# Windowed attention: the value products with a mixed base and stacked half-width corrections

## The chip, the cores and the metric

The kernel runs on one core of one Trainium2 chip. Its time is the device time of one execution in microseconds (us). The core has five engines with a queue of instructions each, worked off in order: PE (TensorE, matrix products; PEld is its weight load), DVE (VectorE), ACT (ScalarE), POOL (GpSimd) and SP (SyncE). In this kernel SP and POOL issue the transfers, which run on 16 DMA engines. The order of each queue is fixed when the program is built; semaphores hold an instruction back until what it reads is there and what it overwrites has been read.

## The reference

One inference step of a hybrid decoder layer for 1024 prompt tokens and 8 x 8 sample tokens with shared weights, all in float32. Cut to what matters here:

```
q, k, v, glu_a, glu_b, gate_a, gate_b = rmsnorm(x) @ w_in
A = attention(q, k, v) @ w_o_attn            # window 128, 16 heads of 64, 4 kv heads, sinks
B = swish(layernorm(conv31(glu_a * sigmoid(glu_b)))) @ w_pb
h = x + (sigmoid(gate_a) * A + sigmoid(gate_b) * B) @ w_out
y = h + ConvFFN(rmsnorm(h))                  # then a final rmsnorm

def swa_prompt(q, k, v, sinks):              # blocks of 128 queries
    # block n attends to the keys of block n-1 and of its own block n
    i, j = arange(128)[:, None], arange(256)[None, :]
    delta = i + 128 - j
    mask = (delta >= 0) & (delta < 128)      # exactly 128 keys for each query
    p = softmax(concat([where(mask, q k^T / 8, -inf), sink]))
    return p[..., :-1] @ v
```

Query i of a block sees the keys 0 to i of its own block and the keys i+1 to 127 of the block before. So each key position 0 to 127 is used exactly once, with one of the two blocks' key and value.

## The kernel before

A float32 product is made of three matmuls: weights and activations are split into a high and a low part (`split_ps`: a cast on ACT, a difference on DVE), and `mm3` (L208, L209, L210) adds high x high, high x low and low x high. The tokens (1024 + 64) stream through a weight in chunks of 384, 384 and 320 columns.

The program has phases. Phase x streams the weights of the input projection over the normed tokens: the convolution inputs (b, a), gates (g), then k, v and q, and between them runs the attention units. Eight units of the prompt (one for each block of 128 queries) and four of the samples are done for each pair p of key heads: p = 0 at about 205 to 366 us of the span, p = 1 at about 445 to 592 us. A unit has steps that hang on an agenda: `values` (the split of the values), and for each of two groups g of four heads `scores`, `turn` (transposes the probabilities p with four matmuls and splits them into `ph` and `pl`, 128 keys x 512 columns, that is 4 heads x 128 queries) and `mix` (the product with the values). `stream` calls `tick` ahead of each three matmuls, and a step is issued when its time on the agenda has come. So its matmuls stand between those of the stream. A scheduler of the framework then sets each engine's order by priorities and dependences.

The values of a block and of the one before meet in this way: `vt[:, 0]` holds the split values of the own block, `vt[:, 1]` the split difference v[blk-1] - v[blk]. `mix` multiplies p with the own values, and adds the product of the difference with that part of p whose key lies in the block before (key position j > i, a mask `below` on the transposed p). For block 0 there is no block before and no correction. With correction, two masked copies `pth0` and `ptl0` (L471, 128 x 512 each on DVE) and four matmuls of 512 columns (L482) are needed for each group, without it two. The corrected ones are 7 blocks x 2 groups x 2 pairs = 28 mixes. Sums of high and low part are taken later: the stationary operand `v` has the high values in one half of its columns and the low ones in the other, so the two halves of the output's partitions are added (L487 on ACT, L488 on DVE).

Beside this, the convolution module: `conv` runs 31 taps on DVE (L582 and others) for each of 8 channel tiles; its result goes to memory in the tile `d_c` by two transfers that POOL issues (L606 with 64 columns, L605 with 1024), and `ln_steps` (the LayerNorm of the branch) loads it back as `ct` (L634, SP), sums squares on DVE (L620) and takes the mean over channels with a matmul on PE (L628, `aux<-sm,mean`). The first such mean stands on PE near 629 us. The gates go out to `d_ga` and `d_gb` (POOL, L804) from `gt`, a copy of the PSUM bank on ACT (L240); they come back as `ga` (SP, L1064), and ACT takes their sigmoid (L1065). The finished attention of p = 0 lies in memory as `d_ah`, `d_al` and comes back as `ah`, `al` (SP, L1018 and L1019) into the space that the attention units leave.

A weight tile is loaded raw (`wraw`, SP, L157, two buffers) and split into `whi` and `wlo` (ACT L179 or L189, with L180 and an adding transfer of POOL, L181, or with DVE L190).

Of the kernel before, what the change touches and what calls it, by code (L numbers as in the profile page):

```python
# [129 lines left out]
class Build:  # L130
# [291 lines left out]
    def attn_unit(self, p, blk, st):  # L422
# [34 lines left out]
        def turn(g):  # L457
            pt = live[g]["pt"]
            ps = self.bank("aux")
            for h in range(4):  # L460
                nc.tensor.transpose(ps[:, h * P:(h + 1) * P], pt[:, h, 0:P], self.ident)  # L461
            ph = self.t(self.at, [P, 512], "pth", F32R)
            pl = self.t(self.at, [P, 512], "ptl", F32R)
            parts = [(0, ph), (0, pl)]
            with self.later(TURN_SOONER if self.now - self.gated <= 3 else 0):
                self.split_ps(ph, pl, ps)
                if blk:
                    below = self.masks[:, None, WIN:2 * WIN].to_broadcast([P, 4, WIN])
                    for x, tag in ((ph, "pth0"), (pl, "ptl0")):
                        x0 = self.t(self.at, [P, 512], tag, F32R)  # L470
                        nc.vector.tensor_tensor(x0.rearrange("p (a b) -> p a b", a=4),  # L471
                                                x.bitcast(F32).rearrange("p (a b) -> p a b", a=4), below, ALU.mult)
                        parts.append((1, x0))
            live[g]["parts"] = parts

        def mix(g):
            r, o = [slice(x * HD, (x + 1) * HD) for x in (g, 1 - g)]
            av = self.bank("aux")
            parts = live[g]["parts"]
            for n, (y, x) in enumerate(parts):  # L480
                v = vals["vt"][:, y, 2 * g:2 * g + 2, :].rearrange("p x d -> p (x d)")
                nc.tensor.matmul(av, v, x, start=n == 0, stop=n == len(parts) - 1)  # L482
            if g == 0:
                live[0]["t"] = self.t(self.at, [P, 4 * P], "av").rearrange("p (a b) -> p a b", a=4)
            t = live[0]["t"]
            av = av.rearrange("p (a b) -> p a b", a=4)
            nc.scalar.copy(t[r], av[o])  # L487
            nc.vector.tensor_tensor(t[r], av[r], t[r], ALU.add)  # L488
            if g == 1:
                self.split_ps(q[0][:, :, qs], q[1][:, :, qs], t)  # L490
# [239 lines left out]
    def phase_x(self):  # L730
# [129 lines left out]
        def do_v():  # L860
            ws = [self.weight(("v", 0)), self.weight(("v", 1))]
            for blk in range(9):
                c = min(blk // 3, 2)
                off = blk * P - CHUNKS[c][0] if blk < 8 else CHUNKS[2][1] - P
                ps = self.bank("mm")
                for k in range(KT):
                    wh, wl = ws[k // 4]
                    kk = slice((k % 4) * 256, (k % 4) * 256 + 256)
                    lh, ll = xh[c][:, k, off:off + P], xl[c][:, k, off:off + P]
                    self.mm3(ps[:, :256], lh, ll, wh[:, kk], wl[:, kk], k == 0, k == KT - 1)  # L870
                if blk < NBLK:
                    nc.scalar.copy(self.v[:, blk].rearrange("p x g d -> p (x g d)"), ps[:, :256])
# [127 lines left out]
        kv = pool(kv_es, "kv")  # L1000
        self.at = pool(kv_es, "at")
        self.v = self.t(kv, [P, NBLK, 2, 2, HD], "v")
        self.masks = self.t(kv, [P, MTOT], "masks")
        nc.sync.dma_start(self.masks, a["masks"])

# [1122 lines left out]
def pack_masks():  # L2128
# [10 lines left out]
    return np.concatenate([above, below, np.where(ok, 0.0, -1e30).astype(np.float32)], 1)  # L2139


def pack_consts(i):
# [81 lines left out]
```

## Time and profile before

| | |
|---|---|
| median of 3 runs | 1638.94 us (1638.71 to 1641.65) |
| profiled execution | 1639.45 us, span 1637.7 us, mean granted clock 0.998 |
| busy PE / DVE / ACT / POOL | 1621.8 / 1369.8 / 901.9 / 301.6 us |
| share of PE in the chain that ended last | 80% |
| idle PE, longest waits | 3.4 us at L628 (for DVE), 2.0 us at L209 (for a weight) |

The profile's times are microseconds from the start of the span. A row of the timeline has start, duration, engine, line, operation, out<-in, shape and number, and in square brackets how long the engine was idle before it and what released it. Matmuls overlap in the records, so their rate is read from the distance of their starts. "SPq" is SP's queue.

### The profile page before, as it was taken

The page shows a single profiled execution, that of the slowest core. Times are in us where ns is not written, and L with a number is a line of the kernel's source. Part 1 is how long each engine was busy: PE and PEld are TensorE (multiplying, and loading weights), DVE is VectorE, ACT ScalarE, POOL GpSimd, SP SyncE. Part 2 cuts the span into 40 slices and gives each one's busy share as a digit, 9 for nine tenths or more (in the row PEclk, how much of TensorE's full clock was granted, in tenths as well). Part 3 has the DMA queues.
Part 4 walks back from the last instruction along what each step waited for, and adds up shares of the span by engine and source line. Part 5 has one row for each costly group of instructions (what it writes and reads, how often), then busy time and mean ns, then how long its engine had stood idle before and what let it go on. Part 6 is the DMA issues. An engine that isn't in the chain of part 4 may idle for free.

```text
span 1637.7 us, 30023 instructions
## 1 busy us (share of the span) xinstructions
PE 1621.8 (99%) x11428; PEld 1602.6 (98%) x11428; DVE 1369.8 (84%) x2463; ACT 901.9 (55%) x1948; POOL 301.6 (18%) x587
## 2 busy tenths in 40 slices
PE   9999999999999999999999999999999999999998
PEld 9999999999999999999999999999999999999998
DVE  7889678999869996788755999988888877889767
ACT  6535387875588754576532465555555555524322
POOL 0210122333112221111102422322222111000000
PEclk9999999999999999999999999999999999999999
DMA  6343433545433366548763632344444334676423
GB/s 211 98 98 90 114 95 97 140 132 143 109 85 78 118 215 202 176 154 232 188 227 102 209 119 72 112 116 118 119 120 109 106 106 157 225 177 160 110 62 110
DMA packets 110329, 221.51 MB, mean 135 GB/s; under 512 B 26600, under 2 KB 57320, under 8 KB 110168
## 3 DMA queue, kind: packets, MB, share of 16 engines
q1 hardware_dynamic: 81528, 131.47, 26.0%
q0 software_dynamic: 28224, 87.71, 20.2%
q8 instruction: 90, 1.47, 0.4%
q14 instruction: 55, 0.45, 0.1%
q10 hardware_dynamic: 432, 0.40, 0.1%
HBM read 137.55 MB, written 64.03 MB: 123 GB/s over the span
## 4 chain that ended last, share of the span: by engine, by line
PE 80%; DVE 8%; DMA 4%; issue 4%; ACT 3%; POOL 0%; SPq 0%; POOLq 0%; DVEq 0%; ACTq 0%
PE mm L208 19%; PE mm L209 19%; PE mm L210 19%; PE aux L210 6%; PE aux L208 6%; PE aux L209 6%; DVE c L582 2%; PE aux L482 1%; DVE bt L582 1%; DVE q L824 1%; PE aux L461 1%; PE aux L449 1%; PE aux L450 1%; DMA ct<-d_c 1%; DMA wlo<-wraw 1%
## 5 line engine op out<-in xcount | busy, mean ns | idle before, releaser
L208 PE MATMUL mm<-xh,whi 128*128 128x384 f32 (+1 forms) x904 | 299.2, 331 | 0.2 <-ACT xh L297 0.2
L209 PE MATMUL mm<-xl,whi 128*128 128x384 f32 (+1 forms) x904 | 296.4, 328 | 0.4 <-DVE xl L298 0.4
L210 PE MATMUL mm<-xh,wlo 128*128 128x384 f32 (+1 forms) x904 | 296.3, 328 | 0.3 <-DMA wlo<-wraw 0.3
L209 PEld LDWEIGHTS mm<-xl,whi 128*128 128x128 f32 x904 | 170.5, 189 | 2.5 <-DVE xl L298 0.9
L208 PEld LDWEIGHTS mm<-xh,whi 128*128 128x128 f32 x904 | 170.5, 189 | 2.0 <-ACT xh L297 0.7
L210 PEld LDWEIGHTS mm<-xh,wlo 128*128 128x128 f32 x904 | 170.2, 188 | 1.1 <-DMA wlo<-wraw 0.7
L1470 DVE SCALAR_TENSOR_TENSOR acc<-st,fc,acc 128x1104 f32<-128x1104 f32 x88 | 119.8, 1364 | 12.2 <-issue 6.7
L582 DVE SCALAR_TENSOR_TENSOR bt<-u,consts,bt 128x513 f32<-128x513 f32 x120 | 89.6, 746 | 3.7 <-ACT bt L592 3.1
L210 PE MATMUL mm<-th,wlo 128*128 128x272 f32 x320 | 92.3, 289 | 0.0
L209 PE MATMUL mm<-tl,wlo 128*128 128x272 f32 x320 | 92.3, 288 | 0.0
L208 PE MATMUL mm<-th,wlo 128*128 128x272 f32 x320 | 92.2, 288 | 0.0
L582 DVE SCALAR_TENSOR_TENSOR c<-sm,hsum,c 128x512 f32<-128x512 f32 x120 | 89.3, 745 | 0.5
L210 PE MATMUL mm<-mh,wlo 128*128 128x272 f32 (+4 forms) x304 | 88.9, 292 | 0.0
L582 DVE SCALAR_TENSOR_TENSOR c<-u,consts,c 128x512 f32<-128x512 f32 x112 | 83.4, 744 | 0.4
L243 ACT CAST whi<-wraw 128x512 fp32r<-128x512 f32 x76 | 47.5, 625 | 62.7 <-PE aux L210 25.7
L1815 ACT COPY st<-mm 128x272 f32<-128x272 f32 (+2 forms) x132 | 43.5, 348 | 54.0 <-PE mm L210 53.8
L243 ACT CAST wlo<-wraw 128x512 fp32r<-128x512 f32 x76 | 47.3, 623 | 40.1 <-DVE wraw L1666 16.6
L1468 ACT ACTIVATE acc<-st,fc 128x1104 f32<-128x1104 f32 x44 | 57.6, 1315 | 14.9 <-DVE st L1771 11.8
L208 PE MATMUL aux<-mh,whi 128*128 128x272 f32 (+4 forms) x216 | 63.8, 295 | 0.0
L209 PE MATMUL aux<-ml,whi 128*128 128x272 f32 (+4 forms) x216 | 63.5, 294 | 0.0
L244 DVE TENSOR_TENSOR wlo<-wraw,wlo 128x512 fp32r<-128x512 f32 x76 | 52.7, 695 | 9.5 <-ACT wlo L243 9.3
L208 PEld LDWEIGHTS mm<-th,wlo 128*128 128x128 f32 x320 | 60.2, 188 | 0.0
(726 smaller groups left out, 5799.2 us busy)
## 6 DMA issues: line engine op xcount, KB each, us to landing
wraw<-wall SPq DMA_DIRECT2D x118, 512.0 KB, 3.8
wlo<-wraw POOLq DMA_DIRECT2D x37, 512.0 KB, 4.5
bw<-d_b SPq DMA_DIRECT2D x42, 272.0 KB, 3.9
d_b<-gd POOLq DMA_DIRECT2D x36, 272.0 KB, 6.1
d_b<-acc POOLq DMA_DIRECT2D x24, 272.0 KB, 4.7
ar<-wdn SPq DMA_DIRECT2D x32, 192.0 KB, 3.8
d_g<-acc POOLq DMA_DIRECT2D x10, 544.0 KB, 4.7
ga<-d_ga SPq DMA_DIRECT2D x8, 544.0 KB, 5.4
```

Source lines behind the costliest of these rows:

```text
L208: mm(ps, wh, xh, start=first, stop=False, skip_group_check=more)
L209: mm(ps, wh, xl, start=False, stop=False, skip_group_check=more)
L210: self.last_mm = mm(ps, wl, xh, start=False, stop=last, skip_group_check=more).ins
L243: self.cast = self.nc.scalar.copy(h, src).ins
L244: self.low = self.nc.vector.tensor_tensor(l, src, h.bitcast(F32), ALU.subtract).ins
L449: nc.tensor.matmul(ps[:, j, :], q[g][:, h, qs], kd[g][:, keys], start=True, stop=False)
L450: nc.tensor.matmul(ps[:, j, :], q[g][:, h, qs], kl[g][:, keys], start=False, stop=True)
L461: nc.tensor.transpose(ps[:, h * P:(h + 1) * P], pt[:, h, 0:P], self.ident)
L582: mac = lambda o, x, w: nc.vector.scalar_tensor_tensor(o, x, w, o, ALU.mult, ALU.add)
L1468: nc.scalar.activation(acc, st[:, 0:AW], AF.Identity, bias=fb(f), scale=fw(f, 0))
L1470: nc.vector.scalar_tensor_tensor(acc, st[:, k:k + AW], fw(f, k), acc, ALU.mult, ALU.add)
L1815: self.evicted = (add if second and n == 0 and j == 1 else op)(d, r(banks[bank, j]))
```

## The change

1. `do_v` makes a second copy of the values, `vw`: the keys 0 to 63 of a block from the own block and the keys 64 to 127 from the block before. For this each block's values are copied out of PSUM twice more, as 64 x 256 on ACT (14 more copies). The base `vt` of a corrected unit is the split of `vw[:, blk]`.
2. With that base, a query of the first half of a block (i < 64) is wrong only for keys j < 64 with j > i, and one of the second half only for keys j >= 64 with j <= i, there with the other sign. So each half of the queries needs a correction over 64 keys alone. The mask table holds this with signs.
3. The 64 rows that `ph` would leave empty take `pl`: `ptc` is the masked `ph` (one operation of 128 x 512), over whose unused half of the partitions the masked `pl` is written, for each query half from the other half of the partitions (two operations of 64 x 256). The queries are laid out half by half (x h q), and `mix` puts them back in order when it splits the result.
4. The difference is split into `vs`, and `two` holds each of its key halves in both halves of the partitions, brought there by four transfers from SBUF to SBUF per unit on SP (64 x 256 float32, 64 KB each; 56 in all).
5. `mix` now has two matmuls of 512 columns with the base (L487, L488) and two of 256 columns with `ptc` and `two` (L491), one for each half of the queries.
6. `do_a` asks for two weights ahead where the next weight is v.

```diff
 values():
-            vt = vals["vt"] = self.t(self.at, [P, 2, 4, HD], "vt", F32R, bufs=2)
-            self.split_ps(vt[:, 0, 0:4:3, :], vt[:, 0, 1:3, :], self.v[:, blk, p])
+            vt = vals["vt"] = self.t(self.at, [P, 4, HD], "vt", F32R, bufs=2)
+            self.split_ps(vt[:, 0:4:3, :], vt[:, 1:3, :], (self.vw if blk else self.v)[:, blk, p])
             if blk:
                 d = self.t(self.at, [P, 2, HD], "vd")
                 nc.vector.tensor_tensor(d, self.v[:, blk - 1, p], self.v[:, blk, p], ALU.subtract)
-                self.split_ps(vt[:, 1, 0:4:3, :], vt[:, 1, 1:3, :], d)
+                s = self.t(self.at, [P, 4, HD], "vs", F32R)
+                self.split_ps(s[:, 0:4:3, :], s[:, 1:3, :], d)
+                two = vals["two"] = self.t(self.at, [P, 2, 4, HD], "two", F32R, bufs=2)
+                for x in range(2):
+                    for y in range(2):
+                        nc.sync.dma_start(two[y * HD:y * HD + HD, x].bitcast(F32), s[x * HD:x * HD + HD].bitcast(F32))
 turn(g):
-                    below = self.masks[:, None, WIN:2 * WIN].to_broadcast([P, 4, WIN])
-                    for x, tag in ((ph, "pth0"), (pl, "ptl0")):
-                        x0 = self.t(self.at, [P, 512], tag, F32R)
-                        nc.vector.tensor_tensor(x0..., x..., below, ALU.mult)
-                        parts.append((1, x0))
+                    c = live[g]["c"] = self.t(self.at, [P, 2, 4, HD], "ptc", F32R)
+                    side = self.masks[:, WIN:2 * WIN].rearrange("p (x q) -> p x q", x=2)
+                    pick = lambda o, x, m: nc.vector.tensor_tensor(o, x.bitcast(F32), m, ALU.mult)
+                    pick(c, ph, side[:, :, None, :].to_broadcast([P, 2, 4, HD]))
+                    for x in range(2):
+                        r, o = [slice(y * HD, (y + 1) * HD) for y in (x, 1 - x)]
+                        pick(c[o, x], pl[r, x], side[r, x, None, :].to_broadcast([HD, 4, HD]))
 mix(g):
-            for n, (y, x) in enumerate(parts):
-                v = vals["vt"][:, y, 2 * g:2 * g + 2, :].rearrange("p x d -> p (x d)")
-                nc.tensor.matmul(av, v, x, start=n == 0, stop=n == len(parts) - 1)
+            nc.tensor.matmul(av, pair(vals["vt"]), flat(ph), start=True, stop=False)
+            nc.tensor.matmul(av, pair(vals["vt"]), flat(pl), start=False, stop=True)
+            if blk:
+                for x in range(2):
+                    nc.tensor.matmul(av[:, x * 256:x * 256 + 256], pair(vals["two"][:, x]),
+                                     live[g]["c"][:, x].rearrange("p h q -> p (h q)"), start=False, stop=True,
+                                     skip_group_check=True)
...
-            self.stream(("a", i), xs, a_evac(u))
+            self.stream(("a", i), xs, a_evac(u), ahead=1 + (self.order[self.w_used + 1][0] == "v"))
...
+                    for r in (slice(0, HD), slice(HD, P)):
+                        if 0 < blk + (r.start > 0) < NBLK:
+                            nc.scalar.copy(flat(self.vw, r), ps[r, :256])
...
-    above, below = [x.astype(np.float32) for x in (jj[:, :WIN] > ii, jj[:, :WIN] < ii)]
+    below = np.where(jj[:, :WIN] < HD, (jj[:, :WIN] < ii) & (ii < HD), -1.0 * ((jj[:, :WIN] >= ii) & (ii >= HD)))
```

The engines' orders are the same in both kernels up to the stream of the weight v. After it they move in these places; a row has the line, the operation, out<-in with the number of the tile, and the shape.

PE, one mix of the last block but one of p = 1 (`pth`, `ptl` are the split probabilities, `ptc` the stacked ones), before and after:

```order
L210 MATMUL mm_6370<-xh_23_107,wlo_754_6110 128x384
L482 MATMUL aux_6418<-pth_6347,vt_6306 128x512
L482 MATMUL aux_6418<-ptl_6348,vt_6306 128x512
L482 MATMUL aux_6418<-pth_797_6351,vt_6306 128x512
L482 MATMUL aux_6418<-ptl_798_6353,vt_6306 128x512
L208 MATMUL mm_6370<-xh_23_107,whi_753_6109 128x384
```

```order
L210 MATMUL mm_6463<-xh_23_107,wlo_756_6197 128x384
L487 MATMUL aux_6511<-pth_6440,vt_6393 128x512
L488 MATMUL aux_6511<-ptl_6441,vt_6393 128x512
L208 MATMUL mm_6463<-xh_23_107,whi_755_6196 128x384
L209 MATMUL mm_6463<-xl_24_108,whi_755_6196 128x384
L210 MATMUL mm_6463<-xh_23_107,wlo_756_6197 128x384
L208 MATMUL mm_6463<-xh_23_107,whi_755_6196 128x384
L209 MATMUL mm_6463<-xl_24_108,whi_755_6196 128x384
L491 MATMUL aux_6511<-ptc_6444,two_6401 128x256
L210 MATMUL mm_6463<-xh_23_107,wlo_756_6197 128x384
L491 MATMUL aux_6511<-ptc_6444,two_6401 128x256
```

The corrections have half the columns, and stand some rows later, between matmuls of the stream.

POOL, near the end of phase x, where the last tile of the convolution goes out (`d_c_59`) among the gates (`d_ga_60`), before and after:

```order
L181 DMA wlo_868_6794<-wraw_6684 128x1024
L804 DMA d_ga_60<-gt_6823 128x384
L606 DMA d_c_59<-u_5426 128x64
L605 DMA d_c_59<-u_5426 128x1024
L804 DMA d_ga_60<-gt_6851 128x384
L804 DMA d_ga_60<-gt_6879 128x320
```

```order
L181 DMA wlo_869_6893<-wraw_6783 128x1024
L815 DMA d_ga_60<-gt_6922 128x384
L815 DMA d_ga_60<-gt_6950 128x384
L617 DMA d_c_59<-u_5495 128x64
L616 DMA d_c_59<-u_5495 128x1024
L815 DMA d_ga_60<-gt_6978 128x320
```

The two transfers of the convolution now stand behind the second of the three gate pieces. On ACT the copy that this piece waits for (`gt_6851` before, `gt_6950` after) stands behind the two sigmoids of `ga` in both kernels.

PE, at the first mean of the LayerNorm (L628 before, L639 after), before and after:

```order
L208 MATMUL mm_6931<-xh_23_107,whi_867_6793 128x384
L209 MATMUL mm_6931<-xl_24_108,whi_867_6793 128x384
L210 MATMUL mm_6931<-xh_23_107,wlo_868_6794 128x384
L628 MATMUL aux_6960<-sm_6893,mean_79 128x272
L208 MATMUL mm_6959<-xh_25_109,whi_867_6793 128x320
L209 MATMUL mm_6959<-xl_26_110,whi_867_6793 128x320
```

```order
L208 MATMUL mm_7058<-xh_25_109,whi_868_6892 128x320
L209 MATMUL mm_7058<-xl_26_110,whi_868_6892 128x320
L210 MATMUL mm_7058<-xh_25_109,wlo_869_6893 128x320
L639 MATMUL aux_7059<-sm_6992,mean_79 128x272
L208 MATMUL mm_7058<-xh_25_109,whi_868_6892 128x320
```

The mean stood ahead of the first matmul of the chunk of 320 columns; now it stands behind fifteen of them. The second mean has moved back by thirteen rows, the third stands where it stood. On SP, one weight load that stood behind the loads of `ct` (L634 before, L645 after) now stands ahead of them, as well as the 56 transfers of `two`, which stand between the weight loads of the units.

More of the change, by code (lines that the diff above doesn't have):

```diff
@@ L489, in mix @@
             if g == 1:
-                self.split_ps(q[0][:, :, qs], q[1][:, :, qs], t)
+                order = lambda x: x[:, :, qs].rearrange("p h (x q) -> p x h q", x=2)
+                self.split_ps(order(q[0]), order(q[1]), t.rearrange("p (x h q) -> p x h q", x=2, h=4))
             if p == 0 and g == 1 and blk in (3, 7):
@@ L1002, in phase_x @@
         self.v = self.t(kv, [P, NBLK, 2, 2, HD], "v")
+        self.vw = self.t(kv, [P, NBLK, 2, 2, HD], "vw")
         self.masks = self.t(kv, [P, MTOT], "masks")
@@ L2132, in pack_masks @@
     ii, jj = r[:, None], np.arange(2 * WIN)[None]
-    above, below = [x.astype(np.float32) for x in (jj[:, :WIN] > ii, jj[:, :WIN] < ii)]
+    above = (jj[:, :WIN] > ii).astype(np.float32)
+    below = np.where(jj[:, :WIN] < HD, (jj[:, :WIN] < ii) & (ii < HD), -1.0 * ((jj[:, :WIN] >= ii) & (ii >= HD)))
     b, t = r // HD, r % NT
@@ L2138, in pack_masks @@
     ok = np.concatenate([past] + new, 1)
-    return np.concatenate([above, below, np.where(ok, 0.0, -1e30).astype(np.float32)], 1)
+    return np.concatenate([above, below.astype(np.float32), np.where(ok, 0.0, -1e30).astype(np.float32)], 1)
 def pack_consts(i):
```

19 lines of the change are left out of this document (9 added, 10 removed).

## The prediction

> **What bounds the kernel.** I read the page's first part, then its chain by engine, then the waits of PE.
>
> ```profile
> span 1637.7 us, 30023 instructions
> PE 1621.8 (99%) x11428; PEld 1602.6 (98%) x11428; DVE 1369.8 (84%) x2463; ACT 901.9 (55%) x1948; POOL 301.6 (18%) x587
> PE 80%; DVE 8%; DMA 4%; issue 4%; ACT 3%; POOL 0%; SPq 0%; POOLq 0%; DVEq 0%; ACTq 0%
> PE aux L628 <- DVE sm L620: 4.7, 2, 3.4
> PE mm L209 <- DMA wlo<-wraw: 2.0, 1, 2.0
> ```
>
> PE is busy for 99% and carries 80% of the chain, so columns taken from PE count, unless PE waits for the same event afterwards. Its two longest waits are one for a weight (2.0 us) and one of 3.4 us at the first LayerNorm mean (L628), after all attention. All that PE saves in the attention units meets that second wait, so the question is whether its event comes earlier too.
>
> **PE's saving.** The price of a matmul is the distance of starts, here of 512 columns (three distances in the four rows from 566.99 to 567.66) and of 256 columns (five distances from 565.64 to 566.23).
>
> ```profile
> 565.64 0.28 PE L450 MATMUL aux<-kl,q 128*128 128x256 f32 x1
> 566.23 0.28 PE L449 MATMUL aux<-kd,q 128*128 128x256 f32 x1
> ...
> 566.99 0.39 PE L482 MATMUL aux<-pth,vt 128*128 128x512 f32 x1
> 567.66 0.47 PE L482 MATMUL aux<-ptl,vt 128*128 128x512 f32 x1
> ```
>
> 0.67 / 3 = 0.223 us for 512 columns and 0.59 / 5 = 0.118 us for 256. A corrected mix saves 2 x (0.223 - 0.118) = 0.21 us, 28 of them 5.9 us, half in each pair's units. The issue of the four matmuls stays. [...]
>
> **What DVE gets.** Before, a corrected group has two masks of 128 x 512 (L471); after, one of 128 x 512 and two of 64 x 256. The nearest row for a half-wide operation is the select of 128 x 256 (L454, two of them from 567.50 to 568.16).
>
> ```profile
> 566.29 0.68 DVE L471 TENSOR_TENSOR pth<-pth,masks 128x512 fp32r<-128x512 f32 x1
> 566.89 0.68 DVE L471 TENSOR_TENSOR ptl<-ptl,masks 128x512 fp32r<-128x512 f32 x1
> 567.50 0.77 DVE L454 COPY_PREDICATED p<-masks,aux 128x256 f32<-128x256 uint32 x2
> 568.16 0.68 DVE L244 TENSOR_TENSOR ptl<-aux,pth 128x512 fp32r<-128x512 f32 x1
> ...
> 472.00:613.60 141.60, 141.26 (x886) 136.32 (x885) 138.22 (x267) 104.47 (x288) 30.43 (x55) 1.00 0.46 131
> ```
>
> A mask costs 0.60 us, two halves 2 x 0.33 = 0.66. That is +0.06 us a mix, +0.8 us in the second pair's 14 mixes; between nothing and 2 x 0.60 for two halves lie -0.6 and +0.6 us a mix, and I keep +0.06, the nearest shape. It matters because of the last row (third busy time: DVE): from 472 to 613.6 us DVE works 138.2 of 141.6 us, and by overlapping records even less is free. So in the second pair PE may run ahead of DVE by 2.95 us only as far as its products then don't wait. In the rows above the last mask ends near 567.5 and its product starts at 567.66, 0.2 us later. After the change the corrections stand five and more rows of 0.17 us behind, which gives about 0.9 us. I take for PE's lead at the end of the attention, 592 us, the value of 5 us: 2.95 of the first pair, which DVE's backlog follows, and two thirds of the second. The ends are 3 and 5.9 us.
>
> ACT's 14 copies of 64 x 256 in the stream of v cost at most one such copy each, 0.38 us, and the row before them shows 2.48 us idle. The split of the difference is only renamed. The 56 transfers of 64 KB come to 3.6 MB.
>
> ```profile
> 197.61 0.38 ACT L872 COPY v<-mm 128x256 f32<-128x256 f32 x1 [2.48 <-PE mm L210]
> wraw<-wall SPq DMA_DIRECT2D x118, 512.0 KB, 3.8
> SPq L1018 <- PE aux L542: 5.1, 1, 5.1
> 595.00:620.00 25.00, 24.67 (x150) 24.34 (x149) 18.62 (x30) 6.71 (x9) 5.34 (x9) 1.00 1.04 350
> ```
>
> That is the volume of seven weight loads among 118, spread over 250 us; I cost them at nothing, with a transfer's 3.8 us for each unit hidden by the whole unit between `values` and `mix`. Should SP hold them behind a weight load that waits for its buffer, that cover is gone (a rival below). `ahead` of two at v moves no row, so it costs nothing; PE's 2.0 us wait for a weight stays.
>
> **What the first LayerNorm mean hangs on.** The chain of waits runs from the convolution's last write to the mean.
>
> ```profile
> 613.92 6.43 DMA d_c<-u
> 620.37 0.37 SPq L634
> 620.79 6.46 DMA ct<-d_c
> 627.37 0.74 DVE u L620
> 629.05 1.24 PE aux L628 x2
> ```
>
> Before, the write starts when DVE ends (613.6) and takes 6.43 us, in a stretch in which the DMA engines are full (the row from 595 to 620: share 1.04, 350 GB/s). That burst is `ah`, `al` and `ga`, and it begins when PE's last sample product lets go of the space (the wait of SP for `aux` L542). After the change, POOL has the write behind the second piece of the gate.
>
> ```profile
> 620.07 1.11 ACT L1065 ACTIVATE ga<-ga 128x1088 f32<-128x1088 f32 x1 [1.23 <-DMA ga<-d_ga]
> 621.09 0.46 ACT L240 COPY gt<-mm 128x384 f32<-128x384 f32 x1
> 621.84 0.54 POOL L804 DMA_DIRECT2D d_ga<-gt  x1 [7.38 <-ACT gt L240]
> 613.92 0.54 POOL L605 DMA_DIRECT2D d_c<-u  x1 [1.26 <-DVE u L603]
> 622.52 1.23 DVE L190 TENSOR_TENSOR wlo<-wraw,whi 128x1024 fp32r<-128x1024 f32 x1 [8.90 <-ACT whi L189]
> d_c<-u POOLq DMA_DIRECT2D x8, 512.0 KB, 2.9
> ```
>
> That piece went out at 621.84, since its copy on ACT waits out both sigmoids, and these the loads of `ga`. So the write is now released by the gate's load, not by DVE. The burst of loads starts 5 us earlier with PE, so the second piece goes out at 616.8, and after it and the small write (0.55 us each) the big write starts at 617.9: 4.0 us later than before. But by then the burst is over. The write takes between 2.9 us (the median of eight) and 6.43; I take 3.5, nearer the median, because one or two weight loads still run. It lands at 621.4 instead of 620.35. On SP a weight load that waits for DVE's L190 now stands ahead of `ct`; it was free at 623.75, 1.9 us after the second piece went out, so by the same shift at 618.7, before the write lands, and costs nothing unless the write is quick. The mean's operand is ready at 629.05 + 1.05 = 630.1.
>
> PE gets there earlier, but now with fifteen matmuls of 320 columns ahead.
>
> ```profile
> 625.35 0.34 PE L210 MATMUL mm<-xh,wlo 128*128 128x384 f32 x1
> 629.05 1.24 PE L628 MATMUL aux<-sm,mean 128*128 128x272 f32 x2 [3.36 <-DVE sm L620]
> 630.36 0.47 PE L209 MATMUL mm<-xl,whi 128*128 128x320 f32 x1
> 630.62 0.47 PE L210 MATMUL mm<-xh,wlo 128*128 128x320 f32 x1
> ...
> 633.07 0.31 PE L209 MATMUL mm<-xl,whi 128*128 128x320 f32 x1
> 633.80 0.31 PE L208 MATMUL mm<-xh,whi 128*128 128x320 f32 x1
> 692.90 0.72 PE L628 MATMUL aux<-sm,mean 128*128 128x272 f32 x2 [1.37 <-DVE sm L620]
> 647.11 1.05 ACT L189 CAST whi<-wraw 128x1024 fp32r<-128x1024 f32 x1 [5.49 <-PE mm L209]
> ```
>
> From 633.07 to 633.80 five distances give 0.146 us each, fifteen rows 2.2 us. PE would come to the mean at 625.7 - 5 + 2.2 = 622.9 and wait 7.2 us instead of 3.4. The sum at this place: the mean 1.05 us later, 2.2 us of work already done, net **1.15 us earlier**. The slow stretch stays: after 3.36 us without work two matmuls stand 0.26 us apart (630.36, 630.62), and from 633.07 on at the latest 0.146; I take the stretch as equally long after the longer wait. [...] The later means follow: the row at 647.11 shows the LayerNorm's ACT work behind a cast that waits for PE, so the chain takes PE's time there; the wait at 692.90 (1.37 us) moves with it.
>
> The sum: 1639.45 - 1.15 = 1638.3 for an execution like the profiled one. The profile lies 0.5 us over the median of 1638.94, so against it **1637.8 us**.
>
> **Rivals.** 0.2% is 3.3 us, about what a measurement of this kernel can tell from no change.
> (B) The saving arrives whole. The DMA queue drains faster than I assume, or the write needs no more than its 2.9 us, and the mean is no later than before by PE's own lead: 1638.94 - 5.9 = 1633.0, with a share of it up to 1635.6. For it speaks that `ga` was late only through the burst; against it that the write has to stand behind the gate, whose time is bounded by PE's lead, and that with the longest lead it lands at 619.9, 0.5 us earlier than now, for 0.5 + 2.2 = 2.7 us in all, 1636.2.
> (C) Slower through the gate: lead only 3 us, the second piece at 618.8, the big write at 619.9 with 6.43 us. It lands at 626.4, 6 us late, less 2.2: 3.8 us slower, 1642.7. It decides from a landing 5.5 us later than 620.35 (3.3 slower). For it: the order on POOL; against it: the burst is then over.
> (D) Slower through `two`: the corrections wait for a transfer or for DVE. The stall must exceed 0.21 us in a mix to lose the gain, and 1.15 + 3.3 = 4.5 us over 14 units, 0.3 us each, would make it slower beyond the noise: 1642.2 and more. PE shows no wait at its mixes before, but DVE has 0.2 us to spare at some.
> (E) The half matmul is no cheaper than two thirds of the full one (0.15 us): saving 28 x 2 x 0.07 = 4 us, PE's lead 3.4; the gate then holds the mean as in my sum with 1.6 us more, 1639.4, no change.
>
> **Chances.** My forecast 0.53, (B) 0.20, (C) 0.09, (D) 0.09, (E) 0.09. All of (B) but a tenth is faster by over 3.3 us and a few of my own case, together 0.23; (C) and (D) count half or more as slower, 0.13; the rest, 0.64, is the same. The range from 1633.6 to 1642.2 leaves out the lower half of (B) and the upper ends of (C) and (D). My own case alone spans 1636.2 (above) to 1640.7 (a write of 6.43 us with the lead of 5: 4.0 late, less 2.2).
>
> **What would show it.** Right: L491 at 0.118 us a row; no waits of PE in 205 to 592 us; the first mean with a wait for DVE of 5 to 9 us, released by the write of `d_c` that POOL issues right behind `d_ga`, at 617 to 619 us; later means within 1 to 2 us of before. Wrong: that mean's wait no longer than before (B), PE waiting at L491 for `two` or `ptc` (D), or the write of `d_c` landing after 625 us (C).

## The result and the profile after

The change made the kernel slower: 1649.93 us (median of 4 runs, 1647.94 to 1651.76) against 1638.83 for the kernel before (4 runs now), a ratio of 1.0064 with a 95% interval of 1.0050 to 1.0078. The forecast was 1637.8. Lines of the changed kernel's page, and below the break the longest waits of its PE:

```profile
span 1648.6 us, 30225 instructions
PE 1623.6 (98%) x11428; PEld 1600.2 (97%) x11428; DVE 1378.0 (84%) x2491; ACT 912.3 (55%) x1965; POOL 305.6 (19%) x587
PE 71%; DVE 13%; DMA 5%; issue 5%; ACT 5%; SPq 1%; POOL 1%; DVEq 0%; POOLq 0%; ACTq 0%
...
PE aux L550 <- ACT av L545: 5.3, 1, 5.3
PE aux L639 <- DVE sm L631: 5.2, 3, 3.7
PE aux L466 <- ACT p L420: 2.6, 1, 2.6
PE aux L488 <- DVE ptl L244: 1.7, 2, 1.4
```

The span grew by 10.9 us. DVE's busy time grew by 8.2 us, PE's share of the chain fell from 80 to 71%, and three waits of PE inside the attention units are new: 5.3 us for ACT's `av`, 2.6 us for the first softmax of the second pair, 1.7 us for `ptl`. The old wait at the LayerNorm mean is still there. So the time was lost where the forecast had PE running ahead: the same matmul of the stream (L208) that started at 592.43 us before now starts at 603.95.

**The halves on DVE.** Timeline of DVE in the changed kernel, then the group of all halves from 205 to 600 us:

```profile
477.94 0.68 DVE L475 TENSOR_TENSOR ptc<-pth,masks 128x512 fp32r<-128x512 f32 x1
478.54 0.28 DVE L399 CUSTOM_DVE_ANT_0 sp<-aux,masks,nm 128x64 f32<-128x64 f32 x1
478.86 0.87 DVE L475 TENSOR_TENSOR ptc<-ptl,masks 64x256 fp32r<-64x256 f32 x2
479.76 0.43 DVE L785 TENSOR_TENSOR u<-mm,u 128x256 f32<-128x256 f32 x1
...
L475 DVE TENSOR_TENSOR ptc<-ptl,masks 64x256 fp32r<-64x256 f32 x56 | 23.5, 420 | 1.7
```

The two halves take 479.76 - 478.86 = 0.90 us, 0.45 each, where the forecast had 0.33. The whole mask that they replace took 0.60. That is 0.30 us for each of 28 mixes, 8.4 us. Besides, the first half starts 0.04 us after the operation before it has ended (478.54 + 0.28 = 478.82), where the whole mask let its successor start 0.08 us before its own end (478.54 against 478.62). Over all 28 pairs this is another 0.11 us each, as picks_not_crossed shows below, so 0.41 us a mix or 11.5 us in all. DVE's busy time, which doesn't count the short pauses between the halves, grew by 8.2 us.

**The transfers of the difference.** ACT in the changed kernel, then PE, then SP's issue of the four transfers, then the wait of ACT summed from 195 to 600 us, and the window after (its last but two number is the granted clock):

```profile
485.53 0.62 ACT L243 CAST q<-av 128x512 fp32r<-128x512 f32 x1
492.48 0.30 ACT L243 CAST vs<-vd 128x128 fp32r<-128x128 f32 x1 [6.32 <-DMA two<-vs]
492.68 0.37 ACT L545 COPY av<-aux 128x256 f32<-128x256 f32 x1
...
493.10 0.80 PE L550 MATMUL aux<-av,vs 128*128 128x128 f32 x2 [5.26 <-ACT av L545]
...
483.40 4.37 SPq L443 DMA_DIRECT2D two<-vs  x4
...
ACT vs L243 <- DMA two<-vs: 15.0, 4, 6.3
...
493.00:500.00 7.00, 6.90 (x38) 6.90 (x39) 5.92 (x13) 5.09 (x20) 1.28 (x2) 0.76 0.18 67
```

The scheduler let `values` run units ahead, as far as buffers allow: the cast at 492.48 belongs to the unit two ahead of the next mix. The cast of `vs` (one buffer) waits until the transfers have read the last `vs`; these could not start before 483.40, when PE had done the last correction that still read the buffer of `two` to be written. Then they took 6.3 to 7.8 us from issue to landing, against a median of 2.4 us for all 56, in a stretch in which the DMA engines were 91 to 97% busy (483 to 489 us) and the adding transfer of a weight, 512 KB, had been issued at 482.08. Behind the cast in ACT's queue stands the copy `av` of a sample unit, and PE waits for that one. After 5.26 us of waiting PE's clock was 0.76 over the next 7 us, another 0.24 x 7 = 1.7 us: it was 0.50 from 493.5 to 496 us and 1.00 from 496.5 to 500. In the kernel before, after the 3.36 us of waiting at the mean, it was 0.50 from 630 to 632 and 1.00 from 633 to 636.

### The profile page after: what moved, and what is told of

Read it like the earlier page. It is cut to its first block, busy times and chain, and to the rows that moved or that the text cites. A ratio compares the mean times of both kernels' runs of the same rounds, so it can differ in the third digit from the quotient of the medians.

```text
span 1648.6 us, 30225 instructions
## 1 busy us (share of the span) xinstructions
PE 1623.6 (98%) x11428; PEld 1600.2 (97%) x11428; DVE 1378.0 (84%) x2491; ACT 912.3 (55%) x1965; POOL 305.6 (19%) x587
## 4 chain that ended last, share of the span: by engine, by line
PE 71%; DVE 13%; DMA 5%; issue 5%; ACT 5%; SPq 1%; POOL 1%; DVEq 0%; POOLq 0%; ACTq 0%
PE mm L208 16%; PE mm L209 16%; PE mm L210 16%; PE aux L210 6%; PE aux L208 6%; PE aux L209 6%; DVE c L593 4%; DVE bt L593 2%; DVE q L835 1%; DMA two<-vs 1%; DMA ct<-d_c 1%; DMA wraw<-wall 1%; ACT ct L673 1%; PE aux L454 1%; ACT p L416 1%
## 5 line engine op out<-in xcount | busy, mean ns | idle before, releaser
L208 PE MATMUL mm<-xh,whi 128*128 128x384 f32 (+1 forms) x904 | 299.1, 331 | 0.0
L208 PEld LDWEIGHTS mm<-xh,whi 128*128 128x128 f32 x904 | 170.7, 189 | 0.7 <-ACT xh L297 0.2
L208 PE MATMUL mm<-th,wlo 128*128 128x272 f32 x320 | 92.2, 288 | 0.0
L208 PE MATMUL aux<-mh,whi 128*128 128x272 f32 (+4 forms) x216 | 63.8, 295 | 0.0
L208 PEld LDWEIGHTS mm<-th,wlo 128*128 128x128 f32 x320 | 60.2, 188 | 0.0
```

Source lines behind the costliest of these rows:

```text
L208: mm(ps, wh, xh, start=first, stop=False, skip_group_check=more)
```

## The experiments

All ratios are to runs of the kernel before on the same chip.

| run | median us | ratio to before (95%) |
|---|---|---|
| pe_alone | 1636.34 | 0.9986 (0.9978 to 0.9995) |
| dve_alone | 1645.90 | 1.0049 (1.0037 to 1.0061) |
| vs_two_buffers | 1650.54 | 1.0068 (1.0053 to 1.0082) |
| four_half_picks | 1654.69 | 1.0100 (1.0086 to 1.0113) |
| two_three_buffers | 1649.52 | 1.0065 (1.0051 to 1.0078) |
| picks_on_pool | 1670.05 | 1.0194 (1.0176 to 1.0211) |
| picks_not_crossed | 1643.29 (one run) | |
| no_transfers | 1643.32 | 1.0027 (1.0018 to 1.0036) |
| held_back | 1647.32 | 1.0062 (1.0049 to 1.0074) |
| full_mask | 1653.73 | 1.0095 (1.0081 to 1.0108) |
| held_and_full | 1641.38 | 1.0022 (1.0013 to 1.0031) |
| moved_by_transfer | 1652.32 | 1.0087 (1.0073 to 1.0100) |
| no_transfers_full_mask | 1635.51 | 0.9980 (0.9971 to 0.9988) |
| held_one_less | 1642.56 | 1.0027 (1.0018 to 1.0036) |
| moved_by_act | 1650.44 | 1.0079 (1.0066 to 1.0091) |
| stacked_by_act | 1645.35 | 1.0049 (1.0035 to 1.0063) |

**pe_alone: only the matmuls.**

```diff
-                nc.tensor.matmul(av, v, x, start=n == 0, stop=n == len(parts) - 1)
+                w = slice(0, 256 if y else 512)
+                nc.tensor.matmul(av[:, w], v, x[:, w], start=n == 0, stop=n > 0, skip_group_check=y > 0)
```

> The kernel before, but each correction matmul covers only the left 256 of its 512 columns (this leaves out the correction of two of the four heads); DVE, ACT, POOL and SP have the same work as before. Theory A (PE's saving is real, the changed kernel lost it elsewhere): 56 matmuls cheaper by 0.10 us save up to 5.9 us on PE, of which the first LayerNorm mean may take back half: 1633 to 1636.5. Rival B (a matmul of 256 columns beside matmuls of 384 costs 0.18 us, as some rows of the changed kernel suggest): 2.5 us at most, 1636.5 to 1638. Rival C (PE's saving is worth nothing because DVE sets the end of the attention): 1638.5 to 1639.5.

Measured: 0.14% faster, 2.3 us of 1638.94, at the edge between theory A's range and rival B's. The price decides for A. A correction in this run, between matmuls of the stream, when its mask is long done:

```profile
563.69 0.34 PE L210 MATMUL mm<-xh,wlo 128*128 128x384 f32 x1
563.87 0.28 PE L483 MATMUL aux<-pth,vt 128*128 128x256 f32 x1
563.98 0.34 PE L208 MATMUL mm<-xh,whi 128*128 128x384 f32 x1
```

It costs 0.11 us, and the median of all 56 (from a correction's start to the start of the next matmul) is 0.118 us, the price forecast. So 256 columns are half the price. The matmul that started at 592.43 us before starts 4.6 us earlier here, near the forecast's lead of 5. POOL and PE at the LayerNorm's mean in the same run:

```profile
616.16 0.54 POOL L805 DMA_DIRECT2D d_ga<-gt  x1 [9.66 <-ACT gt L240]
617.23 0.54 POOL L606 DMA_DIRECT2D d_c<-u  x1
...
629.57 1.25 PE L629 MATMUL aux<-sm,mean 128*128 128x272 f32 x2 [6.22 <-DVE sm L621]
```

Here too the write of `d_c` stands right behind the second gate piece, at 617.23, and PE waits 6.22 us for the mean. This is the forecast's middle part as it was worked out (617.9 and 7.2 us): PE comes earlier, and the mean takes half or more of it back. The order changed here without the change's other parts, by the matmuls alone.

**dve_alone: only more work on DVE.**

```diff
                         parts.append((1, x0))
+                    more = self.t(self.at, [P, 256], "more")
+                    nc.vector.tensor_tensor(more, pl[:, 0:256].bitcast(F32), ph[:, 0:256].bitcast(F32), ALU.mult)
```

> The kernel before, with one more operation of 128 x 256 on DVE behind each pair of masks, written to a tile that nobody reads: 28 x 0.33 = 9.2 us of DVE, about the 8.2 us by which DVE's busy time grew in the changed kernel, and nothing else of the change. Theory A (DVE is the second bound, its work delays the convolutions and with them the second pair's first softmax and the first LayerNorm mean): 1642 to 1648. Rival (DVE had the room, the loss is all in the transfers of the difference): 1638 to 1640.

Measured: 0.49% slower, 7.0 us between the medians, of 9.2 us of added work. Theory A. The way it takes is seen at the end of the sixth convolution, which DVE must finish before the second pair's first softmax. First that row before; then in the changed kernel, with PE's wait for the softmax; then in dve_alone, with PE's waits at the LayerNorm means:

```profile
441.05 0.68 DVE L603 TENSOR_TENSOR u<-c 128x512 f32<-128x512 f32 x1
```

```profile
449.40 0.68 DVE L614 TENSOR_TENSOR u<-c 128x512 f32<-128x512 f32 x1
...
456.33 1.21 PE L466 MATMUL aux<-consts,p 128*128 128x128 f32 x4 [2.64 <-ACT p L420]
```

```profile
449.11 0.69 DVE L605 TENSOR_TENSOR u<-c 128x512 f32<-128x512 f32 x1
...
PE aux L630 <- DVE sm L622: 8.5, 4, 4.8
```

DVE is 8 us late there in both; PE itself is late by 1.5 us there in the changed kernel and by 2.5 in dve_alone, of which 2.0 came with a wait for a weight at 180.81 us, before any unit. The softmax behind it is late, and PE waits for the turn, 2.64 us in the changed kernel and 1.4 in dve_alone; at the LayerNorm means dve_alone waits 8.5 us instead of 4.7.

**vs_two_buffers and two_three_buffers: more buffers.** `vs` gets `bufs=2`; in the second run `two` gets `bufs=3` as well.

> The changed kernel with two buffers for the split difference vs instead of one, so that ACT's next cast need not wait for the four transfers that read the last one. Theory A (this wait, 6.3 us at 486 us, stopped ACT, with it PE for 5.3 us, and cost some 1.5 us of half clock after it): 5 to 7 us faster than the changed kernel, 1643 to 1645. Rival B (the transfers are what is late: PE then waits at L491 for two): 1648 to 1651. Rival C (the loss is DVE's alone): 1648 to 1651 with no wait of PE at L491.

> As vs_two_buffers, with three buffers for two instead of two, so that its transfers no longer wait until PE has done the last correction of two units before (L491, at 483.2 us) and are issued earlier. Theory A (that release held the transfers, these held ACT's cast of vs, and this PE, 5.0 us and some 1.5 us of half clock): no wait of PE at L550, 5 to 7 us faster than the changed kernel, 1643 to 1645.5. Rival (the casts only move ahead by one more unit, as with two buffers of vs, and wait again): 1649 to 1651.

Theory A missed in both: 1650.54 and 1649.52. ACT's cast in two_three_buffers:

```profile
490.78 0.30 ACT L243 CAST vs<-vd 128x128 fp32r<-128x128 f32 x1 [5.48 <-DMA two<-vs]
```

PE still waits 5.0 and 4.4 us at L550 for ACT, which still waits for `two` (6.1 and 5.5 us). The cast that stands there belongs to the unit three ahead of the next mix in vs_two_buffers and four ahead in two_three_buffers, against two in the changed kernel: with each buffer the scheduler moved the casts one unit further ahead, and again one stood on ACT before the same `av`. The rival of two_three_buffers said so; of vs_two_buffers the time fits B and C, but PE didn't wait at L491, and the wait at L550 is not DVE's.

**four_half_picks and picks_not_crossed: the price of a half.** The first, on top of vs_two_buffers, writes the masked `ph` in halves too; the second, on top of two_three_buffers, leaves out the move to the other half:

```diff
-                    pick(c, ph, side[:, :, None, :].to_broadcast([P, 2, 4, HD]))
                     for x in range(2):
                         r, o = [slice(y * HD, (y + 1) * HD) for y in (x, 1 - x)]
+                        pick(c[r, x], ph[r, x], side[r, x, None, :].to_broadcast([HD, 4, HD]))
```

```diff
-                        pick(c[o, x], pl[r, x], side[r, x, None, :].to_broadcast([HD, 4, HD]))
+                        pick(c[r, x], pl[r, x], side[r, x, None, :].to_broadcast([HD, 4, HD]))
```

> As vs_two_buffers, and the masked ph is written as two operations of 64 x 256 into its own half of the partitions instead of one of 128 x 512, so that no operation overwrites what another wrote. Theory A (the halves cost 0.45 us each in the changed kernel because each waits for the one before to have written the same tile; free of that 0.33 us): 4 x 0.33 = 1.32 us instead of 1.50 for each mix, 5 us less DVE, 1 to 4 us faster than vs_two_buffers. Rival (0.45 us is what a half-wide operation costs here): 1.8 us for each mix, 8.4 us more DVE, 3 to 8 us slower than vs_two_buffers.

> As two_three_buffers, but each half of pl is written back to its own half of the partitions (this leaves out the move to the other half, so ptc lacks ph's part and the correction is not the right one); the operations are the same in number, engine and size. It prices the move. Rival A (crossing partitions is what makes 64 x 256 cost 0.44 us instead of 0.33): 0.33 to 0.36 from start to start. Rival B (half the partitions with 256 elements cost this anyway): 0.44.

```profile
477.19 0.40 DVE L475 TENSOR_TENSOR ptc<-pth,masks 64x256 fp32r<-64x256 f32 x1
477.62 0.42 DVE L475 TENSOR_TENSOR ptc<-ptl,masks 64x256 fp32r<-64x256 f32 x1
478.07 0.42 DVE L475 TENSOR_TENSOR ptc<-pth,masks 64x256 fp32r<-64x256 f32 x1
478.53 0.42 DVE L475 TENSOR_TENSOR ptc<-ptl,masks 64x256 fp32r<-64x256 f32 x1
```

```profile
590.75 0.74 DVE L593 SCALAR_TENSOR_TENSOR c<-u,consts,c 128x512 f32<-128x512 f32 x1
591.40 0.86 DVE L475 TENSOR_TENSOR ptc<-ptl,masks 64x256 fp32r<-64x256 f32 x2
592.30 0.68 DVE L498 TENSOR_TENSOR av<-aux,av 64x512 f32<-64x512 f32 x1
```

With four halves (first fence) each takes 0.43 to 0.46 us, and the run is slower: the rival. Not crossed (second fence) the pair still takes 0.90 us, so crossing isn't what makes a half 0.45. But the first half starts at 591.40, 0.09 us before the operation ahead of it ends (590.75 + 0.74); so it is in 27 of 28 pairs, while crossed it starts 0.03 us after that end in all 28. So crossing costs 0.11 us a pair, 3 us in all, and DVE's busy time is 3.3 us less here than in two_three_buffers.

The starts, form by form: crossed, both halves and (in 27 of 28 pairs) the operation behind them start 0.03 us after the one before has ended; not crossed, only the second half and the operation behind do; with four halves, all but the first; and whole masks overlap by 0.08 us (0.60 apart, 0.68 long). Theory A of four_half_picks, that the writes to one tile serialise, doesn't explain why the operation behind the pair, which writes another tile, is held too (479.76 above). What holds them is not shown. The single run of picks_not_crossed lies 6 us under two_three_buffers; the 3 us of DVE may be a part of it, the rest isn't settled.

**picks_on_pool.** The two halves by `nc.gpsimd` instead of `nc.vector`, on top of two_three_buffers.

> As two_three_buffers, with the two operations of 64 x 256 for pl on POOL instead of DVE: 56 x 0.44 = 25 us less on DVE, 16.8 less than in the kernel before. Theory A (DVE's load is what is left of the loss): 5 to 9 us faster than two_three_buffers, 1635 to 1639, if POOL needs no more than 1 us each. Rival (POOL takes several us each, and holds its transfers and PE's corrections behind them): slower than two_three_buffers, PE waiting at L491 for POOL.

```profile
PE aux L491 <- POOL ptc L475: 18.4, 33, 2.9
...
L475 POOL TENSOR_TENSOR ptc<-ptl,masks 64x256 fp32r<-64x256 f32 x50 | 46.2, 924 | 25.0 <-DVE ptc L475 18.4 <-DVE den L406 4.2
```

The rival: 0.92 us each on POOL, with its wait for DVE before, and PE waits 18.4 us at L491.

**no_transfers and no_transfers_full_mask: the two costs apart.** The first, on top of two_three_buffers, gives `vs` itself to the corrections; the second has in addition the mask of full_mask below.

```diff
-                two = vals["two"] = self.t(self.at, [P, 2, 4, HD], "two", F32R, bufs=3)
-                for x in range(2):
-                    for y in range(2):
-                        nc.sync.dma_start(two[y * HD:y * HD + HD, x].bitcast(F32), s[x * HD:x * HD + HD].bitcast(F32))
+                vals["two"] = s
```

> As two_three_buffers, but without the 56 transfers: the corrections take the split difference vs itself as weights (this leaves out the doubling of its halves, so pl is multiplied with the other half's difference). Theory A (with three buffers nothing of the loss is left in the transfers): within 1.5 us of two_three_buffers. Rival (the transfers still cost, through SP's queue or the DMA engines): 3 us faster or more.

> no_transfers with the mask of pl as one operation of 128 x 512 into a tile of its own (this leaves out the doubling of the difference's halves and pl's part of the correction): PE's matmuls as in the changed kernel, DVE's operations as in the kernel before, no transfers. Theory A (the loss is DVE's halves and the transfers, and nothing else): what the matmuls alone gave, 1635 to 1638. Rival (a third cost, such as the corrections' place or the different base): 1640 or more.

1643.32 and 1635.51. Against the kernel before that is +0.27% and -0.20%, and the changed kernel is at +0.64%. So the steps are: matmuls alone -0.20% (-0.14% in pe_alone), DVE's halves +0.47% (+0.49% in dve_alone), transfers +0.37%. In us of 1638.8: -3.3, +7.7 and +6.1. That these add up to the whole is so by construction. What speaks for the split is that each of the first two was measured in a second way that agrees, and that the third is near the 5.3 and 1.7 us of the stall. The second run still has the new base, the copies into `vw` and the corrections at their new place, so none of these is a third cost: its theory A. For no_transfers the rival held, 6.2 us under two_three_buffers: with three buffers the transfers still cost.

**held_back, full_mask, held_and_full: each cost taken out of the changed kernel.** held_back puts the split of the difference behind the previous unit's mix in the order (`self.mixed` is the addition in `mix`); full_mask masks `pl` whole and leaves it out of the correction.

```diff
+                with self.tc.issue_after(self.mixed):
                     d = self.t(self.at, [P, 2, HD], "vd")
...
-                    for x in range(2):
-                        r, o = [slice(y * HD, (y + 1) * HD) for y in (x, 1 - x)]
-                        pick(c[o, x], pl[r, x], side[r, x, None, :].to_broadcast([HD, 4, HD]))
+                    cl = self.t(self.at, [P, 2, 4, HD], "ptd", F32R)
+                    pick(cl, pl, side[:, :, None, :].to_broadcast([P, 2, 4, HD]))
```

> The changed kernel, its buffers as they are, but the split of the difference is put behind the previous unit's mix in the order, so that it can't run units ahead and stand on ACT waiting for transfers that wait for PE. Theory A (the stall near 486 us is ACT's order: the cast waits there for transfers that PE released only at 483 us): no wait of PE at L550, 5 to 7 us faster than the changed kernel, 1643 to 1645. Rival (the transfers come late wherever the cast stands; PE then waits at L491 for two, some 1 us or more in each unit): 1649 or more.

> The changed kernel with pl masked in one operation of 128 x 512 into a tile of its own instead of two of 64 x 256 into ptc (this leaves pl out of the correction). DVE has the same operations as in the kernel before: 0.60 instead of 0.90 us, 28 times, 8.4 us less. Theory A (DVE's load costs the changed kernel what it cost alone, 7 us): 1642 to 1645. Rival (the stall near 486 us covers it: PE waits there anyway): 1647 to 1650.

> Both of these together (pl is left out of the correction, as in full_mask). Theory A (the two costs are separate and there is no third): what the matmuls alone gave, 1635 to 1638.5. Rival (a third cost, such as the waits of the corrections for their mask): 1640 or more.

The waits of PE in held_back (one row) and in full_mask (two rows, and a part of its timeline):

```profile
PE aux L492 <- DMA two<-vs: 4.7, 5, 2.7
```

```profile
PE aux L466 <- ACT p L420: 6.8, 3, 3.8
PE aux L549 <- ACT av L544: 4.9, 1, 4.9
...
316.11 0.30 ACT L243 CAST vs<-vd 128x128 fp32r<-128x128 f32 x1 [5.17 <-DMA two<-vs]
316.31 1.28 ACT L420 ACTIVATE p<-p,den 128x128 f32<-128x128 f32 x4
316.77 1.35 PE L466 MATMUL aux<-consts,p 128*128 128x128 f32 x4 [3.80 <-ACT p L420]
```

held_back: ACT no longer waits, but PE waits 4.7 us for `two` itself, as the rival had it; 1647.32 lies between the two ranges. full_mask missed on the wrong side, 1653.73: the stall for `av` stayed, and one of the same kind came to it in the first pair's units. There ACT's cast waited 5.17 us for `two`, a softmax stood behind it, and PE waited 3.80 us for that softmax, more than half of the 6.8 us at L466; over the next 7 us its clock was 0.76, another 1.7 us. The changed kernel has no wait of PE there. Why DVE's smaller load brought nothing beside this isn't settled; a single edit that also moves the order says little here, and the pairs of runs that agree say more. Both together gave 1641.38, which by time is the rival's: 0.40% under held_back, a third measure of the halves, but 3.6 us above before, where held_back's wait for `two` is left (3.4 us).

**held_one_less: the same transfers, one unit earlier.** As held_back, behind the mix of two units before.

> held_back, but the split of the difference is put behind the mix of two units before instead of one before, so that the transfers have one unit more of time and the cast still can't run further ahead. Theory A (the transfers cost only by their place: ACT waits for them when the cast stands too early, PE when too late): no wait over 1 us of ACT or PE for two, 1642 to 1645, as without transfers. Rival (any place collides): 1646 to 1650, with one of the two waits left.

1642.56, in theory A's range and the time of no_transfers, with no wait of PE for `two` and none at the sample unit's `av`. One wait of ACT is left, near 254 us:

```profile
ACT vs L244 <- DMA two<-vs: 2.5, 1, 2.5
```

It is over theory A's 1 us, but no long wait of PE follows from it. The four transfers issued at 482.57 were no quicker than at the stall (5.4 to 7.0 us); this time no cast had to wait for them. So the transfers' 6 us were their place: ACT waits when the cast stands too early, PE when too late, and one unit earlier than in held_back PE waits for neither. It is the best version that leaves nothing out, 0.37% or 6 us better than the changed kernel by the ratios, and still 0.27% slower than the one before.

**moved_by_transfer, moved_by_act, stacked_by_act: the halves by another way, nothing left out.** The whole mask of `pl` on DVE, then its halves moved by POOL's transfers (on top of held_back) or by copies on ACT (on top of held_one_less); or four copies on ACT and a single mask on DVE.

```diff
+                        nc.gpsimd.dma_start(c[o, x].bitcast(F32), cl[r, x].bitcast(F32))
...
+                        nc.scalar.copy(c[o, x], cl[r, x].bitcast(F32))
...
+                        nc.scalar.copy(m[r, x], ph[r, x].bitcast(F32))
+                        nc.scalar.copy(m[o, x], pl[r, x].bitcast(F32))
+                    pick(c, m, side[:, :, None, :].to_broadcast([P, 2, 4, HD]))
```

> As held_and_full, and the masked pl is then moved into ptc by two transfers of 64 x 256 that POOL issues, 56 in all, so that nothing is left out. Theory A (the transfers are hidden where PE's corrections stand late enough): 1636 to 1640, better than the changed kernel and at best better than the one before. Rival (their latency, about 2.4 us by those of two, is seen by PE at each of 28 mixes): 1645 to 1665, with waits of PE at L491.

> held_one_less with pl masked in one operation of 128 x 512 on DVE and its two halves then copied to the other half of the partitions by ACT (64 x 256, some 0.37 us each, 56 of them, 17 to 21 us more on ACT); nothing is left out. Theory A (DVE's 8.4 us were the loss, and ACT, busy for 125 of 155 us in the second pair's units, has room): 1636 to 1639. Rival (ACT becomes the bound, or the corrections wait for one more engine): 1642 to 1650.

> held_one_less with ptc made by four copies of 64 x 256 on ACT (two of ph in place, two of pl to the other half) and one mask of 128 x 512 on DVE, with a mask table that repeats each half; nothing is left out. DVE has 0.60 us for each mix instead of 1.50, 17 us less than in the kernel before; ACT 33 to 41 us more. Theory A (DVE is the second bound, less of it gains beyond PE's saving): 1633 to 1637. Rival (ACT with up to 150 of 155 us in the second pair's units is the new bound): 1645 to 1665.

1652.32, 1650.44 and 1645.35: the rivals' side each time (moved_by_act 0.44 us above its range). In moved_by_transfer PE waits 5.8 us at its corrections for the moved halves. ACT in the second pair's units (the fourth busy time), first of moved_by_act, then of stacked_by_act:

```profile
445.00:600.00 155.00, 150.26 (x933) 140.66 (x932) 129.10 (x260) 139.27 (x387) 30.19 (x56) 0.99 0.39 102
```

```profile
445.00:600.00 155.00, 152.16 (x955) 142.38 (x954) 129.86 (x257) 145.86 (x414) 28.73 (x53) 1.00 0.40 104
```

ACT is busy for 139 and 146 of 155 us, and in moved_by_act one of its casts again waits 4.1 us for `two`, and PE 3.4 us for the `av` behind it. That ACT's load is what costs here is likely, but not shown. None of the ways tried beats the kernel before.

## Why the prediction was wrong, by its own steps

**PE's saving** (0.21 us a mix, 5.9 us) had the right price: a median of 0.118 us for a correction in pe_alone. In the changed kernel it was not all paid out, because corrections there wait for their half masks on DVE, where the prediction saw 0.9 us of room. (Of the 0.2 us that it read for the kernel before, its rows give 0.1: 566.89 + 0.68 = 567.57, and the product starts at 567.66.) Their median is 0.160 us and the mean 0.171, against a mean of 0.125 in pe_alone: 56 x 0.046 = 2.6 us. With whole masks (no_transfers_full_mask) the median is 0.118 again, with the halves and no transfers 0.179. One case, with the weight load of the second correction:

```profile
579.71 0.34 PE L209 MATMUL mm<-xl,whi 128*128 128x384 f32 x1
579.89 0.34 PE L491 MATMUL aux<-ptc,two 128*128 128x256 f32 x1
580.06 0.34 PE L210 MATMUL mm<-xh,wlo 128*128 128x384 f32 x1
580.29 0.39 PE L491 MATMUL aux<-ptc,two 128*128 128x256 f32 x1
580.51 0.34 PE L208 MATMUL mm<-xh,whi 128*128 128x384 f32 x1
...
580.29 0.19 PEld L491 LDWEIGHTS aux<-ptc,two 128*128 128x128 f32 x1 [0.15 <-DVE ptc L475]
```

From 579.71 to 580.51 are 0.80 us for two stream matmuls (0.35) and two corrections, which makes 0.23 each, as much as 512 columns. Small waits like this one aren't in the list of long waits. They do what rival (E) had, by another cause.

**What DVE gets** is a step that failed by size. The half mask was priced by the select of 128 x 256 at 0.33 us, "the nearest shape", and took 0.45. The ends given for it (-0.6 and +0.6 us a mix) held the true +0.30, or +0.41 with what is lost ahead of the pair, 8.4 or 11.5 us in all; but the sum took +0.06, +0.8 us for the second pair, and the 4.2 us or more of the first pair's units went into no term. The shape had the right number of elements per partition and twice the partitions, and what was priced is an operation whose successor starts 0.11 us before it has ended (567.50 + 0.77 = 568.27 against 568.16), where each half is followed by one that starts 0.03 us after its end. By the runs this step cost some 7 us (0.40 to 0.49%).

**The transfers at nothing** is the step that failed by kind. Their cover was named as PE's, the unit between `values` and `mix`, and that cover can be had (PE has no wait for them in held_one_less). The queue that had to wait was ACT's, because the order put the next cast behind them, ahead of work that PE needs. By the runs this step cost 6 us. Rival (D) had it, "the corrections wait for a transfer or for DVE", with 0.09; for DVE the place was right, for the transfers it was ACT and not the corrections.

**The LayerNorm mean** was right as a mechanism: in pe_alone it took back half or more of PE's lead of 4.6 us. But the lead of 5 us that this term started from did not exist in the changed kernel, by the two steps above: PE was 11.5 us late at 592 us. The chain of waits there:

```profile
628.62 0.46 POOL d_c L617
629.15 5.52 DMA d_c<-u
634.81 0.38 SPq L645
635.24 5.69 DMA ct<-d_c
642.73 0.78 PE aux L639 x2
```

The write goes out right behind the gate piece (628.10), as forecast, but takes 5.52 us and not 3.5, and the mean stands at 642.73, 13.7 us later than before. The slow stretch was as long after a longer wait as the prediction took it to be: PE's clock was 0.76 over 629 to 636 us before (a wait of 3.36 us) and 0.76 over 493 to 500 us after (5.26 us).

The chances (0.13 for slower) rested on one error in common: each extra instruction was priced by its own duration, and none by what stands behind it in its queue.

## What to carry to other kernels

Where the second engine is busy for 98% of a stretch, a change that trades its time for the first engine's must be priced there first: 0.3 to 0.4 us more on DVE for each mix cost 7 us, 0.2 us less on PE brought 2 to 3. A transfer whose source buffer is soon rewritten is a wait on the engine that rewrites it (up to 6.3 us at once on ACT, 15.0 us in four waits): look at what stands behind that instruction in its queue, and fix how far it may run ahead; in both runs with more buffers the scheduler only ran it further.

## What the runs showed of the hardware that was not expected

The halves of 64 partitions x 256 elements took 0.45 us each on DVE from start to start, whether moved to the other half of the partitions or not, against 0.60 for 128 x 512, so that two halves cost one and a half wholes. Where the first of a pair read from one half of the partitions and wrote to the other, it started 0.03 us after the end of the operation before it; where it did not, 0.08 us ahead of that end (27 of 28 pairs): moving cost 0.11 us more a pair. On POOL the same half took 0.92 us.
